# A fused attention and expert layer on one core: which pool holds the projection weights, and where the values stage keeps its gated units

## The chip, the cores and the metric

The kernel runs on one core of a Trainium2 chip. The metric is the time of one execution in microseconds (us). Times are compared as medians of several executions. Engines are named as the profile names them: PE (matmuls) with its weight loads PEld, DVE, ACT, POOL, and SP, which here only issues DMAs.

## The reference

One layer of an encoder is applied to two sequences, a prompt of 512 tokens and a sample of 256, with the same weights (width 1024):

```python
n = rms_norm(x, attn_norm_g)
proj = n @ w_in                    # q, k, v of 8 heads A and 4 heads B
o_a = dilated_attention(...)       # 8 heads of 64
o_b = diff_attention(...)          # 4 heads, two maps each, values of 128
x = x + concat(o_a, o_b) @ w_out
h = rms_norm(x, ffn_norm_g)
# expert layer: 128 * 128 experts of one neuron each
q  = h @ w_q                       # 8 heads, two halves of 128
sc = q . sub_keys                  # 128 scores per half, top 16 of each
best, pos = top_k(pairwise sums of the two lists, 16)
g = softmax(best)
x = x + sum over picks of g * gelu(h . u[e]) * v[e]
```

## The kernel before

Tokens are worked on in tiles of 128: four of the prompt (0 to 3), two of the sample (4, 5). fp32 products are made from three matmuls of split operands: `split` (L71 to L73) casts a raw tile to a rounded high part on ACT (L72) and subtracts it for the low part on POOL or DVE (L73), and `mm3` (L67 to L69) multiplies high by high, high by low and low by high. The stages, in the order in which they come:

1. Norm, input projection and attention of the sample, then of the prompt. `project` (L133) streams a weight matrix in pieces of 128x512 (`wraw`, split into `wh`, `wl`) from the pool `wpool`, three buffers of each.
2. The sample's output projection, its second norm, and its routing: `route_keys` and `route_pairs` find the 16 picks of each head by DVE operations. Routing of tiles 4 and 5 is scheduled beside the prompt's attention. Its last part (L515 to L527) lives in a pool `sr` on the left side: one-hot masks `ei`, `ej` (L491, L493), their sums (L522 to L525), and the expert numbers `eidx` (L526, L527).
3. The prompt's output projection: the first 512 columns of `w_out` by `project` (L536), accumulators `pacc` in four banks, added to the residual by `evac` (L292, DVE); then the other 512 columns from `woh`, `wol` (L541 to L545), second norm and transposes (L127) into `x2p`, two tiles of 16 KB per partition with the tags x0 and x1.
4. The prompt's routing, interleaved with the first `hidden` units: `hidden(j)` loads 128 experts' u vectors (`raw8`, L572), splits them, makes 24 matmuls `pu` with `x2p`, and writes the gelu to DRAM (`h_d`, L593).
5. The gate stage: dense gates of all prompt tokens and experts by one-hot matmuls `pg`, written to DRAM (`g_d`). Then the remaining `hidden` units.
6. The values stage (L677 on): 64 units of two experts' blocks. A unit reads `h_d` into `gw` (L684), multiplies it by gates `gblk` (L669, one 2 MB read for four units; L686), splits the product into `wh`, `wl` (the gated unit) and makes 96 matmuls `py` with two blocks of v. In the second unit the residual (`x1y`, 2 MB) is read back and added by transposes (L694 to L699).

Beside stages 4 to 6 the sample's picks are gathered row by row by POOL's DMAs, with DVE making the dot products (L722 to L732).

What sets the order: the program is written in stage order, and a scheduler that simulates a timeline places each instruction on its engine's queue. An engine's queue runs in order. Pools are stacks of memory, one growing from the left, one from the right; a tile of a pool that is opened where another pool has been closed waits, tile by tile, for the last instructions that used the memory below it. Before the change `wpool` is the upper pool on the right, open from the start until after stage 3. The values stage's pool `dp` (right) holds `gblk`, `gw`, `wh` and `wl`, and is opened at L663, where `wpool` and the prompt's pools have been closed.

Of the kernel before, what the change touches and what calls it, by code (L numbers as in the profile page):

```python
# [11 lines left out]
F32 = mybir.dt.float32  # L12
F32R = mybir.dt.float32r
# [8 lines left out]
P = 128  # L22
D = 1024
# [15 lines left out]
DENSE = 4  # L39
# [12 lines left out]
def tile_kernel(ctx, tc, xs_in, relb, onehot, logm, g1, w_in, gqk, lamv, gdiff, w_out, g2,  # L52
                w_q, skT, uT, uv, out_p, out_s, dbg=None):
    nc = tc.nc
    V, S, G, T = nc.vector, nc.scalar, nc.gpsimd, nc.tensor

    def f(ap):
        return ap.bitcast(F32)

    def pool(stack, name, bufs=1, side="left", **kw):  # L60
        return stack.enter_context(tc.tile_pool(name=name, bufs=bufs, side=side, reuse_waits="tile", **kw))

    def psum(stack, name, bufs):
        return stack.enter_context(tc.tile_pool(name=name, bufs=bufs, space=PSUM, reuse_waits="tile"))

    def mm3(ps, ah, al, bh, bl, start, stop):
        T.matmul(ps, ah, bh, start=start, stop=False)  # L67
        T.matmul(ps, ah, bl, start=False, stop=False)  # L68
        T.matmul(ps, al, bh, start=False, stop=stop)  # L69

    def split(hi, lo, raw, low=None):  # L71
        S.copy(hi, raw)  # L72
        return (low or G).tensor_tensor(lo, raw, f(hi), op=OP.subtract)  # L73
# [3 lines left out]
    late = pool(ctx, "late")  # L77
# [5 lines left out]
    ps_tr = psum(fps, "ps_tr", 1)  # L83
    ps_tr2 = psum(fps, "ps_tr2", 1)
    ps_mm = psum(fps, "ps_mm", 2)
    attm = ctx.enter_context(ExitStack())
    att = pool(attm, "att", 3)
    left = ctx.enter_context(ExitStack())
    ppS = pool(left, "ppS", 3)
    right = ctx.enter_context(ExitStack())  # L90
    ppP = pool(right, "ppP", 3, side="right")
    wpool = pool(right, "wpool", 3, side="right")

    def bank(p, name):
        return p.tile([P, 512], F32, tag="b", name=name)
# [182 lines left out]
    def mixed(n, mix, pp):  # L278
        mh = pp.tile([P, DC, n * P], F32R, tag="pj", name="mh")
        ml = pp.tile([P, DC, n * P], F32R, tag="pj", name="ml")  # L280
        for d in range(DC):
            split(mh[:, d], ml[:, d], mix[d // 4][:, d % 4], G if d < 4 else V)
        return mh, ml

    def residual(t0, n, pp):
        x1 = pp.tile([P, n, D], F32, tag="pj", name="x1")
        for i in range(n):
            nc.sync.dma_start(x1[:, i], xs_in[(t0 + i) * P:(t0 + i + 1) * P, :])

        def evac(i, nb, ps):  # L290
            c = slice(nb * 512, (nb + 1) * 512)
            V.tensor_tensor(x1[:, i, c], ps, x1[:, i, c], op=OP.add)  # L292

        return x1, evac
# [35 lines left out]
    for m in range(2):  # L330
        c = slice(m * 512, (m + 1) * 512)
# [195 lines left out]
        V.tensor_copy(eidx[t], ijf[:, 0])  # L527
    left.close()
    attm.close()


    rw = pool(ctx, "rw", 2)
    mh, ml = mixed(4, mixP, ppP)
    x1, evac = residual(0, 4, ppP)
    obanks = (ps_sc, ps_sc2, ps_tr, ps_tr2)
# [4 lines left out]
    for d in range(DC):  # L540
        raw = wpool.tile([P, 512], F32, name="wraw")  # L541
        nc.sync.dma_start(raw, w_out[d * P:(d + 1) * P, 512:])
        wh = wo.tile([P, 512], F32R, name="woh")
        wl = wo.tile([P, 512], F32R, name="wol")
# [22 lines left out]
    right = ctx.enter_context(ExitStack())  # L567
# [95 lines left out]
    dp = pool(ctx, "dense", 2, side="right")  # L663
    py = [ps_y.tile([P, 512], F32, name=f"py{c}") for c in range(DC)]
    vrows = uv.rearrange("(i j) d -> j i d", j=NK)

    def gates(jb):
        gblk = dp.tile([P, DENSE * P // TB, JB, TB], F32, name="gblk")
        nc.sync.dma_start(gblk, g_d[:, :, jb * JB:(jb + 1) * JB, :].rearrange("b i j t -> i b j t"))  # L669
        return gblk  # L670

    def values_of(j):
        vr, vh, vl = weights8(vrows[j, :, D:].rearrange("i (c d) -> i c d", d=P))
        low_of[NK + j] = split(vh, vl, vr, V)
        return vh, vl

    for jp in range(NK // 2):  # L677
        jj = 2 * jp % JB
        wh = dp.tile([P, 2, 512], F32R, name="wh")
        wl = dp.tile([P, 2, 512], F32R, name="wl")  # L680
        if jj == 0:
            gblk = gates(2 * jp // JB)
        ge = dp.tile([P, 2, 512], F32, name="gw", bufs=3)
        nc.sync.dma_start(ge, h_d[jp])  # L684
        ge4 = ge.rearrange("p k (b t) -> p k b t", t=TB)
        V.tensor_tensor(ge4, ge4, gblk[:, :, jj:jj + 2].rearrange("p b k t -> p k b t"), op=OP.mult)  # L686
        split(wh, wl, ge, V)
        vv = [values_of(2 * jp + k) for k in range(2)]
        for c in range(DC):
            for k, (vh, vl) in enumerate(vv):  # L690
                mm3(py[c], vh[:, c], vl[:, c], wh[:, k], wl[:, k],
                    jp == 0 and k == 0, jp == NK // 2 - 1 and k == 1)
        if jp == 1:
            x1y = late.tile([P, DENSE, D], F32, tag="x0", name="x1y")  # L694
            for t in range(DENSE):
                nc.sync.dma_start(x1y[:, t], x1_d[t])
            for c in range(DC):
                for t in range(DENSE):
                    T.matmul(py[c][:, t * P:(t + 1) * P], x1y[:, t, c * P:(c + 1) * P], ident, start=False, stop=False)  # L699
# [90 lines left out]
```

## Time and profile before

| | |
|---|---|
| median of 3 executions | 2289.11 us (2288.76 to 2289.37) |
| profiled execution | 2282.11 us, of it span 2280.3 us |
| PE busy | 2170.0 us, 95% of the span |
| DVE busy | 1800.5 us, 79% |
| ACT, POOL busy | 915.4 us (40%), 851.3 us (37%) |
| chain that ended last, by engine | PE 66%, DVE 10%, issue 8%, DMA 8%, POOL 5%, ACT 2% |
| DMA over the span | 617.65 MB, mean 271 GB/s |

The span runs from the first to the last instruction that the profiler recorded; the profiled execution's time is 1.8 us more than its span. The busy shares are averages over stages. Of the page's 40 slices of 57 us, PE is at 6 or 7 tenths in the first, the ninth and tenth (456 to 570 us) and the 25th (1368 to 1425 us), and at 8 or more in all others.

### The profile page before, as it was taken

What the parts mean: (1) busy time and instruction counts of PE and PEld (TensorE: products, weight loads), DVE (VectorE), ACT (ScalarE), POOL (GpSimd) and SP (SyncE); (2) the same over time, 40 slices, a digit from 0 to 9 for tenths busy, and PEclk for the clock granted to TensorE, in tenths of its full rate; (3) what the DMA queues carried; (4) which work ended last, traced back from release to release, by engine and by line L of the source; (5) the groups of instructions that cost most, each with busy time, mean ns of one, the idle gap of its engine ahead of it and who ended that gap; (6) DMA issues with size and microseconds to landing.
All of it is one profiled execution on the core that took longest, in us unless ns stands there. A gap on an engine that the chain in (4) does not pass through costs nothing.

```text
span 2280.3 us, 31093 instructions
## 1 busy us (share of the span) xinstructions
PE 2170.0 (95%) x11312; PEld 1770.3 (78%) x11312; DVE 1800.5 (79%) x3500; ACT 915.4 (40%) x1484; POOL 851.3 (37%) x634
## 2 busy tenths in 40 slices
PE   6999999976999989999999997999999999999998
PEld 4788789855887777878888875888878778788876
DVE  5645378997699999989999965666788878888885
ACT  4755587632322234545555532332223222223222
POOL 4767776632456532222322322221222322222320
PEclk9999999988999999999999998999999999999999
DMA  5533353314477776789998899898999999999994
GB/s 187 185 107 123 92 154 94 105 47 161 168 255 261 262 269 227 284 304 348 342 350 329 342 384 387 296 349 288 367 347 364 359 343 372 384 365 360 359 342 177
DMA packets 198681, 617.65 MB, mean 271 GB/s; under 512 B 16016, under 2 KB 82192, under 8 KB 163712
## 3 DMA queue, kind: packets, MB, share of 16 engines
q1 hardware_dynamic: 139968, 278.70, 35.2%
q0 software_dynamic: 36864, 268.45, 31.0%
q10 hardware_dynamic: 21696, 68.53, 7.8%
q8 instruction: 88, 1.44, 0.2%
q14 instruction: 65, 0.53, 0.1%
HBM read 542.17 MB, written 73.45 MB: 270 GB/s over the span
## 4 chain that ended last, share of the span: by engine, by line
PE 66%; DVE 10%; issue 8%; DMA 8%; POOL 5%; ACT 2%; SPq 0%; ACTq 0%; POOLq 0%; DVEq 0%
PE py L67 10%; PE py L68 10%; PE py L69 10%; PE pu L67 6%; PE pu L69 6%; PE pu L68 6%; DMA row<-in_uv_dram,eidx 3%; PE pacc L68 3%; PE pacc L69 3%; PE pacc L67 3%; POOL row L722 2%; DMA raw<-in_uT_dram 2%; PE pg L650 2%; PE pq L69 2%; POOL lo L73 1%
## 5 line engine op out<-in xcount | busy, mean ns | idle before, releaser
L722 POOL DMA_INDIRECT row<-in_uv_dram,eidx x256 | 413.6, 1616 | 1150.8 <-DVE acc L732 1011.1
L72 ACT CAST hi<-raw 128x1024 fp32r<-128x1024 f32 x272 | 285.1, 1051 | 571.7 <-PE pu L68 199.5
L67 PE MATMUL pu<-x2p,hi 128*128 128x512 f32 x1024 | 409.3, 400 | 15.7 <-ACT hi L72 15.6
L69 PE MATMUL pu<-x2p,lo 128*128 128x512 f32 x1024 | 408.5, 399 | 11.0 <-DVE lo L73 7.5
L67 PE MATMUL py<-wh,hi 128*128 128x512 f32 x1024 | 405.2, 396 | 2.6 <-ACT hi L72 2.6
L68 PE MATMUL pu<-x2p,hi 128*128 128x512 f32 x1024 | 406.5, 397 | 0.0
L73 DVE TENSOR_TENSOR lo<-raw,hi 128x1024 fp32r<-128x1024 f32 x236 | 287.7, 1221 | 149.4 <-ACT hi L72 112.5
L68 PE MATMUL py<-wl,hi 128*128 128x512 f32 x1024 | 404.2, 395 | 0.0
L724 DVE CUSTOM_DVE_ANT_0 row<-row,st 128x1024 f32<-128x1024 f32 x256 | 332.1, 1305 | 51.4 <-DMA row<-in_uv_dram,eidx 51.1
L732 DVE SCALAR_TENSOR_TENSOR acc<-row,wgt,acc 128x1024 f32<-128x1024 f32 x256 | 328.8, 1284 | 5.2
L69 PE MATMUL py<-wh,lo 128*128 128x512 f32 x1024 | 303.3, 395 | 0.0
L67 PEld LDWEIGHTS pu<-x2p,hi 128*128 128x128 f32 x1024 | 195.4, 191 | 58.7 <-ACT hi L72 16.9
L69 PEld LDWEIGHTS pu<-x2p,lo 128*128 128x128 f32 x1024 | 194.8, 190 | 55.1 <-DVE lo L73 12.2
L67 PEld LDWEIGHTS py<-wh,hi 128*128 128x128 f32 x1024 | 191.9, 187 | 53.8 <-ACT hi L72 6.9
L69 PEld LDWEIGHTS py<-wh,lo 128*128 128x128 f32 x1024 | 191.9, 187 | 46.9
L68 PEld LDWEIGHTS py<-wl,hi 128*128 128x128 f32 x1024 | 192.0, 187 | 46.3
L68 PEld LDWEIGHTS pu<-x2p,hi 128*128 128x128 f32 x1024 | 195.1, 191 | 38.6
L653 ACT COPY gb<-pg 128x512 f32<-128x512 f32 x128 | 132.7, 1146 | 81.8 <-PE pg L650 80.8
L73 POOL TENSOR_TENSOR wl<-wraw,wh 128x512 fp32r<-128x512 f32 x96 | 127.6, 1335 | 76.3 <-ACT wh L72 72.4
L72 ACT CAST wh<-gw 128x1024 fp32r<-128x1024 f32 x64 | 67.1, 1049 | 174.5 <-PE py L69 162.7
L729 ACT ACTIVATE wgt<-h 128x2 f32<-128x2 f32 x128 | 26.1, 204 | 220.6 <-DVE h L724 219.3
L650 PE MATMUL pg<-og,oij 128*128 128x128 bf16 x1536 | 110.0, 221 | 4.6 <-DVE og L643 4.6
(303 smaller groups left out, 3659.7 us busy)
## 6 DMA issues: line engine op xcount, KB each, us to landing
raw<-in_uT_dram SPq DMA_DIRECT2D x128, 512.0 KB, 5.9
raw<-in_uv_dram SPq DMA_DIRECT2D x128, 512.0 KB, 7.9
h_d<-ge ACTq DMA_DIRECT2D x128, 256.0 KB, 5.6
g_d<-gb ACTq DMA_DIRECT2D x16, 2048.0 KB, 9.4
gblk<-g_d SPq DMA_DIRECT2D x16, 2048.0 KB, 16.5
gw<-h_d SPq DMA_DIRECT2D x64, 512.0 KB, 9.1
wraw<-in_w_in_dram SPq DMA_DIRECT2D x96, 256.0 KB, 2.8
toe<-bias_d SPq DMA_DIRECT2D x24, 448.0 KB, 4.1
```

Source lines behind the costliest of these rows:

```text
L67: T.matmul(ps, ah, bh, start=start, stop=False)
L68: T.matmul(ps, ah, bl, start=False, stop=False)
L69: T.matmul(ps, al, bh, start=False, stop=stop)
L72: S.copy(hi, raw)
L73: return (low or G).tensor_tensor(lo, raw, f(hi), op=OP.subtract)
L650: T.matmul(pg[:, c], oij[:, 0, c4 * 4 + c], og[k][:, c4 * 4 + c], start=k == 0, stop=k == 2)
L653: S.copy(gb[:, :, o:o + 4].rearrange("p j t -> p t j"), pg)
L722: G.indirect_dma_start(out=r, out_offset=None, in_=uv, in_offset=bass.IndirectOffsetOnAxis(ap=eidx[t][:, b + k:b + k + 1], axis=0))
L724: dot = V.tensor_tensor_reduce(r[:, :D], r[:, :D], x2r[t], 1.0, 0.0, OP.mult, OP.add, h[:, k:k + 1])
L729: S.activation(wgt, h, AF.Gelu)
L732: V.scalar_tensor_tensor(acc, rows[k][:, D:], wgt[:, k:k + 1], acc, op0=OP.mult, op1=OP.add)
```

## The change

The diff has three parts.

- `wpool` moves from the right side to the left. It is opened before the attention's pool `att`, in a stack of its own (`wx`) that is closed after `attm`. The prompt's output projection uses a new pool, `wout`, which is opened on the right after the pool `rw`, with the same buffers.
- The gated units of the values stage no longer have tiles of their own in `dp` (two buffers each of `wh` and `wl`). They take the halves `[:, jp % 2]` of two tiles `w0`, `w1`, which have the tags x0 and x1, the buffers of `x2p`.
- `x1y`, which had the tag x0, is now a tile of `dp`.

```diff
     ps_mm = psum(fps, "ps_mm", 2)
+    wx = ctx.enter_context(ExitStack())
+    wpool = pool(wx, "wpool", 3)
     attm = ctx.enter_context(ExitStack())
     att = pool(attm, "att", 3)
...
     ppP = pool(right, "ppP", 3, side="right")
-    wpool = pool(right, "wpool", 3, side="right")
...
     left.close()
     attm.close()
+    wx.close()
...
     rw = pool(ctx, "rw", 2)
+    wpool = pool(right, "wout", 3, side="right")
     mh, ml = mixed(4, mixP, ppP)
...
     for jp in range(NK // 2):
         jj = 2 * jp % JB
-        wh = dp.tile([P, 2, 512], F32R, name="wh")
-        wl = dp.tile([P, 2, 512], F32R, name="wl")
+        wh, wl = (late.tile([P, 2, 2, 512], F32R, tag=f"x{i}", name=f"w{i}") for i in range(2)) if jp == 0 else (wh, wl)
...
-        split(wh, wl, ge, V)
+        gh, gl = wh[:, jp % 2], wl[:, jp % 2]
+        split(gh, gl, ge, V)
...
-                mm3(py[c], vh[:, c], vl[:, c], wh[:, k], wl[:, k],
+                mm3(py[c], vh[:, c], vl[:, c], gh[:, k], gl[:, k],
                     jp == 0 and k == 0, jp == NK // 2 - 1 and k == 1)
         if jp == 1:
-            x1y = late.tile([P, DENSE, D], F32, tag="x0", name="x1y")
+            x1y = dp.tile([P, DENSE, D], F32, name="x1y", bufs=1)
```

Line numbers of the changed kernel are higher by 1 from L94 on, by 3 from L533 on, and by 2 or 3 in the values stage. Below, the names are those of the program; the number behind a name is that of the buffer.

ACT's queue at the end of the prompt's attention, before. `mh` is the last mixed head, `wh` the pieces of `w_out`, `hi8` the first blocks of stage 4, `gate5` the sample's second routing (tile 5):

```order
L72 CAST mh_6406<-mixP_2957 128x512
L72 CAST wh_6489<-wraw_6487 128x512
L72 CAST hi8_6859<-raw8_6857 128x1024
L72 CAST wh_6507<-wraw_6505 128x512
L72 CAST hi8_6893<-raw8_6891 128x1024
L72 CAST wh_6525<-wraw_6523 128x512
L72 CAST wh_6543<-wraw_6541 128x512
L463 ACTIVATE gate5_5201<-gate5_5201 128x128
L72 CAST wh_6561<-wraw_6559 128x512
L72 CAST woh_6586<-wraw_6584 128x512
```

The same place of ACT's queue now:

```order
L72 CAST mh_6410<-mixP_2957 128x512
L72 CAST hi8_6863<-raw8_6861 128x1024
L72 CAST hi8_6897<-raw8_6895 128x1024
L464 ACTIVATE gate5_5201<-gate5_5201 128x128
L72 CAST wh_6439<-wraw_6437 128x512
L72 CAST wh_6457<-wraw_6455 128x512
L72 CAST wh_6475<-wraw_6473 128x512
L72 CAST wh_6493<-wraw_6491 128x512
```

Before, three `wh` stand far ahead of these rows, four between `mh` and `gate5`, and one behind it; now all eight stand behind `gate5`. PE's queue follows: of the 96 matmuls `pacc<-wh,mh` and the like, 27 stood between the matmuls of the last attention head, and now all 96 stand behind its last transpose (L271, now L272). On DVE the four `wol` subtractions and the four residual additions of the first half stood among the routing of tile 5; now they stand behind its last operation.

SP's queue with what each DMA waits for, the first pieces of `w_out` now. A wait names the engine or the DMA queue whose count is waited for:

```order
L575 DMA raw8_7003<-in_uT_dram 128x1024 [waits DMAHW6_49,DMAHW3_49,Pool_49]
L575 DMA raw8_7038<-in_w_q_dram 128x8x128 [waits DMAHW7_49,DMAHW4_49,Pool_49]
L140 DMA wraw_6437<-in_w_out_dram 128x512 [waits DMAHW0_49,DVE_49]
L140 DMA wraw_6455<-in_w_out_dram 128x512 [waits DMAHW1_49,PE_49]
L140 DMA wraw_6473<-in_w_out_dram 128x512 [waits DMAHW2_49]
L140 DMA wraw_6491<-in_w_out_dram 128x512 [waits DMAHW0_49,Pool_49]
```

Before, the pieces waited for POOL alone (the subtraction that frees a buffer), and the first six were loaded during the attention. In the compiled program the count of DVE that `wraw_6437` waits for is that of L494 (L493 before), the multiplication of tile 5's `ej`; the first cast `wh_6439` waits for L526 (L525 before) and the second for L528 (L527), the sum and the last cast of the same tile.

SP's queue at the end of the gate stage before, where the values stage's first reads go out between the blocks of the hidden units:

```order
L669 DMA gblk<-g_d 128x16x256
L684 DMA gw<-h_d 128x1024 x3
L669 DMA gblk<-g_d 128x16x256
L572 DMA raw_14332<-in_uT_dram 128x1024
L572 DMA raw_14366<-in_uT_dram 128x1024
L572 DMA raw_14400<-in_uT_dram 128x1024
L684 DMA gw<-h_d 128x1024 x2
L572 DMA raw_14434<-in_uT_dram 128x1024
L572 DMA raw_14468<-in_uT_dram 128x1024
L572 DMA raw_14502<-in_uT_dram 128x1024
L669 DMA gblk<-g_d 128x16x256
L572 DMA raw_14536<-in_uT_dram 128x1024
```

And now:

```order
L672 DMA gblk<-g_d 128x16x256
L686 DMA gw<-h_d 128x1024 x2
L699 DMA x1y<-x_d_97 128x1024
L699 DMA x1y<-x_d_98 128x1024
L699 DMA x1y<-x_d_99 128x1024
L699 DMA x1y<-x_d_100 128x1024
L686 DMA gw<-h_d 128x1024
L575 DMA raw_14336<-in_uT_dram 128x1024
L672 DMA gblk<-g_d 128x16x256
L575 DMA raw_14370<-in_uT_dram 128x1024
L575 DMA raw_14404<-in_uT_dram 128x1024
L575 DMA raw_14438<-in_uT_dram 128x1024
```

Two `gw` and the third `gblk` move from here to behind the first blocks of v; the four reads of `x1y` came from there. The casts of the first two gated units stood on ACT among the hidden units; now they stand behind the last gelu, and in the compiled program the cast of the third unit still waits for the last matmul of the first.

## Rows read from the trace of the kernel before

**Rows 1.** busy time of the engines, from the page

```profile
PE 2170.0 (95%) x11312; PEld 1770.3 (78%) x11312; DVE 1800.5 (79%) x3500; ACT 915.4 (40%) x1484; POOL 851.3 (37%) x634
```

**Rows 2.** PE's timeline, 474 to 557 us: start, length, engine, line, operation, [idle before]

```profile
474.35 0.80 PE L67 MATMUL pacc<-wh,mh 128*128 128x512 f32 x1 [2.41 <-DVE mx L195]
...
521.38 1.68 PE L67 MATMUL pacc<-wh,mh 128*128 128x512 f32 x4 [2.63 <-ACT wh L72]
...
532.66 0.77 PE L67 MATMUL pacc<-woh,mh 128*128 128x512 f32 x1 [6.40 <-DVE x L292]
...
553.64 0.40 PE L67 MATMUL pacc<-woh,mh 128*128 128x512 f32 x1
...
556.21 0.40 PE L69 MATMUL pacc<-woh,ml 128*128 128x512 f32 x1
```

**Rows 3.** DVE's timeline, the sample's routing, 470 to 543 us

```profile
470.04 0.45 DVE L470 CAST tb<-ti 128x256 bf16<-128x256 uint32 x1
...
497.95 0.27 DVE L468 TENSOR_TENSOR gate<-gate,gr 128x128 f32<-128x128 f32 x1
...
503.00 1.20 DVE L493 TENSOR_TENSOR ej<-ej,tb 128x2048 bf16<-128x2048 bf16 x1
...
506.43 2.49 DVE L470 CAST tb<-ti 128x256 bf16<-128x256 uint32 x1
...
523.21 2.29 DVE L493 TENSOR_TENSOR ei<-ei,di 128x2048 bf16<-128x2048 bf16 x1
...
538.74 2.21 DVE L493 TENSOR_TENSOR ej<-ej,tb 128x2048 bf16<-128x2048 bf16 x1
540.99 1.48 DVE L524 TENSOR_TENSOR ej<-ej 128x1024 bf16<-128x1024 bf16 x3
542.50 0.29 DVE L525 TENSOR_TENSOR ijf<-ej 128x128 f32<-128x128 bf16 x1
```

**Rows 4.** PE's waits, 1340 to 1430 us: total, times, longest

```profile
PE pu L67 <- ACT hi L72: 15.6, 3, 6.1
```

**Rows 5.** windows: length, busy PE, PEld, DVE, ACT, POOL (instructions), PE clock, DMA share, GB/s

```profile
1350.00:1390.00 40.00, 28.21 (x107) 21.57 (x107) 23.92 (x29) 10.42 (x15) 6.63 (x4) 0.87 1.04 399
1420.00:1430.00 10.00, 4.28 (x10) 2.81 (x10) 3.85 (x7) 2.15 (x4) 0.00 (x0) 0.66 0.78 290
1430.00:1500.00 70.00, 70.00 (x311) 57.95 (x310) 48.29 (x58) 21.78 (x33) 20.65 (x13) 1.00 0.86 325
```

**Rows 6.** ACT's timeline, one cast at 521 us, two operations near 1550 us

```profile
520.72 0.60 ACT L72 CAST wh<-wraw 128x512 fp32r<-128x512 f32 x1
...
1543.19 0.59 ACT L592 ACTIVATE ge<-pu 128x512 f32<-128x512 f32 x1
...
1555.14 1.05 ACT L72 CAST wh<-gw 128x1024 fp32r<-128x1024 f32 x1
```

**Rows 7.** DVE by line, 500 to 544 us: count, busy us, mean ns, idle before

```profile
L524 DVE TENSOR_TENSOR ej<-ej 128x1024 bf16<-128x1024 bf16 (+2 forms) x6 | 5.5, 915 | 0.1
...
L73 DVE TENSOR_TENSOR wol<-wraw,woh 128x512 fp32r<-128x512 f32 x4 | 2.9, 736 | 1.1 <-ACT woh L72 1.1
L292 DVE TENSOR_TENSOR x<-pacc,x 128x512 f32<-128x512 f32 x4 | 2.5, 676 | 0.0
...
L525 DVE TENSOR_TENSOR ijf<-ej 128x128 f32<-128x128 bf16 x2 | 1.5, 762 | 0.0
...
L468 DVE TENSOR_TENSOR gate<-gate,gr 128x128 f32<-128x128 f32 x1 | 1.3, 1316 | 0.0
```

**Rows 8.** POOL's timeline, 505 to 524 us

```profile
505.92 2.85 POOL L73 TENSOR_TENSOR lo<-raw,hi 128x1024 fp32r<-128x1024 f32 x1
...
521.40 1.74 POOL L73 TENSOR_TENSOR wl<-wraw,wh 128x512 fp32r<-128x512 f32 x1 [6.24 <-ACT wh L72]
```

**Rows 9.** DMA issues, 500 to 545 us: KB each, us to landing

```profile
wraw<-in_w_out_dram SPq DMA_DIRECT2D x10, 256.0 KB, 2.7
```

**Rows 10.** window of the second half, same columns

```profile
532.60:556.60 24.00, 23.94 (x96) 18.95 (x96) 11.40 (x19) 2.36 (x5) 4.00 (x3) 0.94 0.26 99
```

## The prediction

> **What bounds the kernel now.** First the page: PE is busy for 2170.0 of 2280.3 us [rows 1], so PE's queue sets the end nearly everywhere, and the question is where the change adds idle time on PE or takes some away. The profiled execution took 2282.1 us, 7.0 less than the median of 2289.1; I make the sum against 2282.1 and add 7.0 at the end. Then PE's timeline around the place where the diff moves `w_out`. The reader is to see three things in it [rows 2]: at 474.35 us PE already makes matmuls of the prompt's output projection in a gap of the attention (it had idled 2.41 us for DVE); the first half still runs at 521.38, after a small wait for ACT; the second half starts at 532.66, after 6.40 us of waiting for the residual additions on DVE, and its last matmul starts at 556.21 and ends at 556.6. Then DVE in the same stretch: it works through the sample's routing, and the last multiplication of tile 5's `ej` starts only at 538.74 [rows 3]. Last come the waits and windows at the end of the gate stage, where PE waits 15.6 us for casts of blocks that are late [rows 4, 5], and ACT around 1543 to 1555 us, where the hidden units end [rows 6].
>
> **Part one: the output projection behind the routing (slower).** The new pool `wout` lies on memory of the sample's routing. The first `wraw` now waits for DVE's multiplication of tile 5's `ej`; SP's queue stands behind it, and ACT's first `wh`, POOL's `wl` and all 192 matmuls `pacc` come after. Queued behind the waiting read on SP are the other pieces and then stage 4's reads, five blocks of which stand ahead of it; behind ACT's waiting cast are the pieces and the norm of the same stage. So only this stage waits. Before, the weights waited for no part of the routing. So I need the end of that multiplication in the new order.
>
> It ended at 538.74 + 2.21 = 540.95 [rows 3]. Ahead of it stood four `wol` subtractions (2.9 us and 1.1 us of waiting for ACT) and four residual additions (2.5 us), 6.5 us in all [rows 7], which now come after it. That alone gives 534.45.
>
> Besides, DVE operations of the routing take longer while POOL makes its low parts: the multiplications of L493 at 523.21 and 538.74 took 2.29 and 2.21 us against 1.20 at 503.00; the six additions of L524 took 5.5 us together, where three at 540.99, with POOL quiet, took 1.48; L525 1.5 for two against 0.29 for one; L468 1.3 against 0.27 [rows 3, 7]. Over the undisturbed durations that is 2.1 + 2.5 + 0.9 + 1.0 = 6.5 us. POOL's `wl` and `wol`, as the one at 521.40 [rows 8], go behind the routing with the weights, so I take these 6.5 us off too: 527.9. Bounds: nothing comes off (534.45), or 2.0 more does, if the cast at 506.43 (2.49 us against 0.45 at 470.04 [rows 3]) is freed of the `lo` of 505.92 [rows 8], which stays on POOL: 525.9.
>
> [...]
>
> From there: 2.7 us for the `wraw` to land [rows 9]; 0.6 us for the cast of `wh` [rows 6]; PE starts at 531.2. A half of the projection, 96 matmuls, took 23.94 us with its slow start after a wait [rows 10]; so I take the first half from 531.2 to 555.1, since the pieces (cast 0.6, POOL below 2 us, three buffers) come faster than twelve matmuls, some 2.9 us, use them up. One of the four additions, 0.63 us [rows 7], is exposed before the second half. The second half runs warm: the twelve matmuls from 553.64 to 556.21 start 0.234 us apart [rows 2], so 96 take 22.4 us. The end is 555.1 + 0.6 + 22.4 = 578.1 against 556.6: **21.5 us later**, bounds 19.5 and 28. PE idles from the end of the attention to 531 and nothing else is on its queue: the 27 matmuls that filled gaps of the last head fill none now. What follows (norm, transposes, prompt's routing) begins with the last matmul of this stage, so it shifts as a whole.
>
> **Part two: fewer early reads at the end of the gate stage (faster, small).** In full-speed stretches a matmul slot is 70/311 = 0.225 us. From 1350 to 1390 us there were 107, so 40 − 107 × 0.225 = 15.9 us were lost, and from 1420 to 1430 10 − 10 × 0.225 = 7.7 us [rows 5], part of it at a granted clock of 0.87 and 0.66 of full speed. The DMA rate there is 399 GB/s, at a busy share of 1.04 [rows 5], so what the early reads cost is their bytes. Before, these were three `gblk` and five `gw`, 8.5 MB; now they are two `gblk`, three `gw` and `x1y`, 7.5 MB. One MB less at 399 GB/s is 2.5 us: **2.5 us earlier**. Ahead of the first block stand 5.5 MB both times, so the first loss stays. The bounds: the 7.7 us behind the third `gblk` go whole, or nothing is won, since the two `gw` and the `gblk` now go out at the start of the values stage, with 1 MB more than `x1y` there, worth 2.5 us if that stretch waits for DMA: −7.7 to +2.5.
>
> **Part three: hidden to values (slower, small).** `w0` lies on `x2p`, so the first gated unit is cast only after the last `pu`. The last gelu, 0.59 us, stands before the cast of 1.05 us on ACT [rows 6], and PE waits for both: **1.6 us later**. The low part on DVE is hidden behind the first eight matmuls with the high part. Bounds 0 (the gelu's wait hides behind a wait for a block) and 5 (the stage begins with three gated reads instead of five in hand). In the steady stage the halves take turns as the two buffers did: the cast of a unit waits for the matmuls two units back, as before; cost nothing, hidden behind a unit of 96 matmuls.
>
> **Sum.** 21.5 − 2.5 + 1.6 = 20.6; 2282.1 + 20.6 + 7.0 = 2309.7 us.
>
> **Rivals.**
> Routing with no relief: DVE's lengthening is not POOL's doing, `ej` ends at 534.45, and part one costs 28. Then 2316. For it: most lengthened rows are of tile 5, whose data may differ; against it the three quick additions at 540.99, of tile 5 too [rows 3].
>
> Not slower: the wait for the routing decides nothing. Place: the first `wraw`. Price nil if the multiplication of `ej` ends before 527.9 − 21.5 = 506.4; the point from which it costs is there. Then 2282.1 − 2.5 + 1.6 + 7.0 = 2288.2, and faster by over 0.2% only if part two also wins its 7.7 (2283). Against it: in DVE's queue the routing of tile 5 can't be done at 506, where DVE is only at its first cast [rows 3].
>
> The early reads win everything: both losses of part two, 23.6 us, go, and the time is 2288.6, no change. For it: the third `gblk` is gone from there; against it: 5.5 MB still stand ahead of the first block.
>
> The values stage loses its lead: with fewer gated reads in hand, and 3 MB of reads at its start, its first units wait for theirs. At 5 us for each of two units it is 10 us: 2320. For it: the reads are larger there than before; against it: they are behind the first five blocks of v, and used two units, over 20 us, later. That the halves do not do what they say (a unit waiting for the other half's matmuls) would add a cast, 1.05 us, to each of 62 units, 2375; the waits in the program speak against it.
>
> **How the numbers follow.** Forecast 0.70, for 2303 to 2315; no relief 0.12; values stage worse 0.08; halves 0.01; not slower at the projection 0.05; early reads win all 0.04. The range holds the forecast and the no-relief case, with some of the values case: 2299 to 2320. About 0.2% (4.6 us) is what a measurement of this kernel can tell from no change; of the last two cases faster by more gets 0.04 and within it 0.05, the others are slower, 0.91.
>
> **What would show it.** In the profile of the changed kernel: the first `pacc` with `wh` at about 531 (no earlier than 3 us after L494 of tile 5), PE idle for over 25 us before it, and the last with `woh` near 578; DVE's L494 and L525 of tile 5 near 1.2 us and 1.5 us for three; PE's wait for the cast of `hi` near 1420 gone and that near 1370 not; one wait of about 1.6 us at the first `py`; and no new waits in the values stage. I am wrong if `pacc` begins before 515, or if PE waits in the values stage exceed 5 us.

## The result

The changed kernel took 2303.82 us (median of 7 runs, 2298.21 to 2314.86), the kernel before 2289.11 (7 runs, 2283.25 to 2292.93). The ratio is 1.0069, with a 95% interval of 1.0046 to 1.0091: by the ratio slower by 16 us, between 10.5 and 21. The forecast was 2309.7 us, range 2299 to 2320.

The profiled execution of the changed kernel took 2314.86 us, the longest of its seven. Its span was 32.7 us longer than that of before, twice the difference of the medians, so a second profile was taken (e12 below, 2304.79 us). Where PE stood at the ends of the stages in the two kernels, read from PE's timeline (us from the span's start):

| | last `woh` matmul ends | last `pg` ends | last `pu` ends | first `py` | last `py` ends | span |
|---|---|---|---|---|---|---|
| before | 556.6 | 1333.6 | 1542.4 | 1542.3 | 2271.6 | 2280.3 |
| changed, first profile | 577.1 | 1359.0 | 1571.8 | 1574.1 | 2304.2 | 2313.0 |
| changed, second profile | 574.8 | 1351.3 | 1565.4 | 1567.8 | 2294.2 | 2303.0 |

The output projection costs 20.5 us in the first and 18.2 in the second profile, the hidden stage 4.0 and 5.3, the step from `pu` to `py` 2.5, and the values stage +0.8 and −2.9. The stretch between the projection and the last `pg` differs by 4.9 and −0.5, in which I see the spread of single executions. Counted from the end of the attention's last transposes (500.3 us before, 503.1 and 500.8 after), the projection ends 56.3 us later before, and 74.0 us later in both profiles after: 17.7 us more.

The page after, whose lines answer to [rows 1]: PE has lost 11 us of busy time, though it makes the same matmuls.

```profile
span 2313.0 us, 31093 instructions
...
PE 2159.4 (93%) x11312; PEld 1779.3 (77%) x11312; DVE 1791.0 (77%) x3500; ACT 915.4 (40%) x1484; POOL 835.9 (36%) x634
```

PE's timeline after, the lines that answer to [rows 2]: one wait of 26.66 us stands between the last transpose of the attention and the first matmul of the projection, and the 96 matmuls of a half follow one another.

```profile
501.99 1.12 PE L272 MATMUL pt<-ident,on 128*128 128x128 f32 x4 [9.15 <-DVE on L269]
529.76 2.08 PE L67 MATMUL pacc<-wh,mh 128*128 128x512 f32 x4 [26.66 <-ACT wh L72]
...
554.45 0.50 PE L67 MATMUL pacc<-woh,mh 128*128 128x512 f32 x1 [0.29 <-DVE x L293]
...
576.72 0.40 PE L69 MATMUL pacc<-woh,ml 128*128 128x512 f32 x1
```

DVE's and POOL's timelines after, which answer to [rows 3] and [rows 8]. The multiplication of tile 5's `ej` (L494 now) takes 1.23 us, not 2.21; the first `wl` waits for the cast of 529.1. Beside the two `lo` at 505.50 other operations are stretched than before: L526 takes 2.29 us there, and 0.29 at 527.66.

```profile
503.90 0.29 DVE L471 CAST tb<-ti 128x256 bf16<-128x256 uint32 x1
...
505.98 2.29 DVE L526 TENSOR_TENSOR ijf<-ej 128x128 f32<-128x128 bf16 x1
...
508.41 2.21 DVE L527 SCALAR_TENSOR_TENSOR ijf<-ijf 128x128 f32<-128x128 f32 x1
...
524.89 1.23 DVE L494 TENSOR_TENSOR ej<-ej,tb 128x2048 bf16<-128x2048 bf16 x1
526.15 1.48 DVE L525 TENSOR_TENSOR ej<-ej 128x1024 bf16<-128x1024 bf16 x3
527.66 0.29 DVE L526 TENSOR_TENSOR ijf<-ej 128x128 f32<-128x128 bf16 x1
```

```profile
505.50 4.97 POOL L73 TENSOR_TENSOR lo<-raw,hi 128x1024 fp32r<-128x1024 f32 x2 [6.49 <-ACT hi L72]
529.79 3.75 POOL L73 TENSOR_TENSOR wl<-wraw,wh 128x512 fp32r<-128x512 f32 x3 [19.31 <-ACT wh L72]
```

PE's waits after, 1340 to 1600 us, which answer to [rows 4]: four waits for casts of blocks, not three, and two new ones at the start of the values stage.

```profile
PE pu L67 <- ACT hi L72: 18.5, 4, 10.4
PE py L67 <- ACT w L72: 2.3, 1, 2.3
PE pu L69 <- DVE lo L73: 1.5, 1, 1.5
PE py L68 <- DVE w L73: 1.1, 1, 1.1
```

At that start ACT casts a block of v ahead of the last gelu, and DVE makes two dot products of the sample's gathers ahead of the first low part `w` (ACT's timeline, then DVE's; the lines answer to [rows 6]):

```profile
1571.56 1.04 ACT L72 CAST hi<-raw 128x1024 fp32r<-128x1024 f32 x1 [3.90 <-PE pu L68]
1572.51 0.59 ACT L595 ACTIVATE ge<-pu 128x512 f32<-128x512 f32 x1
1573.00 1.04 ACT L72 CAST w<-gw 128x1024 fp32r<-128x1024 f32 x1
```

```profile
1573.78 1.22 DVE L727 CUSTOM_DVE_ANT_0 row<-row,st 128x1024 f32<-128x1024 f32 x1
...
1574.93 1.22 DVE L727 CUSTOM_DVE_ANT_0 row<-row,st 128x1024 f32<-128x1024 f32 x1
...
1576.07 2.35 DVE L73 TENSOR_TENSOR w<-gw,w 128x1024 fp32r<-128x1024 f32 x2
```

Windows of 100 us in the values stage (columns as in [rows 5]), before and then after. Before, 428 matmuls take 99.75 us of PE's time, 0.233 each. After, a window almost without waits has 437 in 99.44, 0.228 each; the one ahead of it holds 409, since PE idles 5.5 us there.

```profile
1600.00:1700.00 100.00, 99.75 (x428) 79.86 (x427) 78.96 (x92) 28.68 (x35) 24.29 (x16) 1.00 0.96 352
```

```profile
1700.00:1800.00 100.00, 94.54 (x409) 77.36 (x408) 78.25 (x91) 28.03 (x34) 24.79 (x17) 0.98 0.93 356
1800.00:1900.00 100.00, 99.44 (x437) 81.38 (x436) 82.73 (x96) 29.01 (x36) 26.97 (x17) 1.00 0.96 366
```

PE's waits from 1700 us to the end after: 15.4 us for casts of blocks, where the kernel before had 1.7 in the same part.

```profile
PE py L67 <- ACT hi L72: 15.4, 12, 5.2
```

### The profile page after: what moved, and what is told of

It is laid out like the page before. It is cut to its first block, busy times and chain, and to the rows that moved or that the text cites. A ratio compares the mean times of both kernels' runs of the same rounds, so it can differ in the third digit from the quotient of the medians.

```text
span 2313.0 us, 31093 instructions
## 1 busy us (share of the span) xinstructions
PE 2159.4 (93%) x11312; PEld 1779.3 (77%) x11312; DVE 1791.0 (77%) x3500; ACT 915.4 (40%) x1484; POOL 835.9 (36%) x634
## 4 chain that ended last, share of the span: by engine, by line
PE 64%; DMA 12%; DVE 10%; issue 8%; POOL 4%; ACT 2%; SPq 0%; ACTq 0%; POOLq 0%; DVEq 0%
PE py L67 8%; PE py L68 8%; PE py L69 8%; PE pu L67 6%; PE pu L69 6%; PE pu L68 6%; DMA raw<-in_uv_dram 4%; PE pacc L68 3%; DMA row<-in_uv_dram,eidx 3%; PE pacc L69 3%; PE pacc L67 3%; POOL row L725 2%; DMA wraw<-in_w_in_dram 2%; PE pg L653 2%; PE pq L69 2%
## 5 line engine op out<-in xcount | busy, mean ns | idle before, releaser
L725 POOL DMA_INDIRECT row<-in_uv_dram,eidx x256 | 399.0, 1559 | 1179.3 <-DVE acc L735 1041.8
L67 PE MATMUL py<-w,hi 128*128 128x512 f32 x1024 | 400.9, 393 | 18.4 <-ACT hi L72 15.9
L68 PE MATMUL py<-w,hi 128*128 128x512 f32 x1024 | 400.4, 391 | 1.1 <-DVE w L73 1.1
L69 PE MATMUL py<-w,lo 128*128 128x512 f32 x1024 | 294.2, 389 | 0.4 <-DVE lo L73 0.4
L67 PEld LDWEIGHTS py<-w,hi 128*128 128x128 f32 x1024 | 193.2, 189 | 66.1 <-ACT hi L72 23.6
L68 PEld LDWEIGHTS py<-w,hi 128*128 128x128 f32 x1024 | 193.4, 189 | 41.4 <-DVE w L73 1.6
L69 PEld LDWEIGHTS py<-w,lo 128*128 128x128 f32 x1024 | 192.1, 188 | 40.7 <-DVE lo L73 0.8
L72 ACT CAST w<-gw 128x1024 fp32r<-128x1024 f32 x64 | 67.0, 1049 | 168.4 <-PE py L69 167.7
L72 ACT CAST wh<-wraw 128x512 fp32r<-128x512 f32 x120 | 74.4, 623 | 104.0 <-DMA wraw<-in_w_in_dram 38.7
```

Of the source, the lines that this page charges most:

```text
L725: G.indirect_dma_start(out=r, out_offset=None, in_=uv, in_offset=bass.IndirectOffsetOnAxis(ap=eidx[t][:, b + k:b + k + 1], axis=0))
```

## The experiments

Ratios are to the kernel before on the same chip in the same hours.

**e3, the first part alone** (`wpool` on the left, `wout` on the right; values stage as before).

```diff
+    wx = ctx.enter_context(ExitStack())
+    wpool = pool(wx, "wpool", 3)
...
-    wpool = pool(right, "wpool", 3, side="right")
...
+    wx.close()
     rw = pool(ctx, "rw", 2)
+    wpool = pool(right, "wout", 3, side="right")
```

> Only the first part of the change: projection weights on the left, the output projection's on the right behind the attention; the values stage as before. Theory of the prediction: the first matmul of the output projection with wh waits until about 530, and the whole time is 20 us above before, less 2 to 4 us of faster input projection: 2305 to 2310; py stays at 0.234. If the loss lies elsewhere: 2289 within 5.

2309.59 us, ratio 1.0090 (1.0069 to 1.0110): +20.6 us by the ratio. PE's timeline has the wait (26.75 us), and the projection ends at 573.5 against 556.6, 16.9 us later (18.4 counted from the end of the attention). In this profile the values stage is longer too, 735.2 us against 729.3, so that not all of the 20.6 need be the projection's:

```profile
525.56 2.08 PE L67 MATMUL pacc<-wh,mh 128*128 128x512 f32 x4 [26.75 <-ACT wh L72]
```

**e4, the changed kernel with `wout` on the left.**

```diff
     rw = pool(ctx, "rw", 2)
-    wpool = pool(right, "wout", 3, side="right")
+    wox = ctx.enter_context(ExitStack())
+    wpool = pool(wox, "wout", 3)
...
-    wox = ctx.enter_context(ExitStack())
     wo = pool(wox, "wo", DC)
```

> The changed kernel, with the pool of the output projection's weights opened on the left, below wo, so that it lies on memory of the attention and not of the sample's routing. Theory of the prediction: the first wraw no longer waits for the multiplication of tile 5's ej; the projection starts soon after the attention, 0 to 8 us later than before (no pieces ahead of time), and the whole time is 12 to 20 us below the changed kernel: 2284 to 2292. If the wait for the routing was not the cause: 2304 within 4.

2287.46 us, ratio 0.9991 (0.9970 to 1.0012), 16 us below the changed kernel. PE's timeline: the wait is 1.95 us, and the projection ends at 564.0, 7.4 us behind before. With e3 this shows the wait for the routing to be what makes the changed kernel slow: it comes with the place of the pool, and goes with it.

```profile
506.14 2.07 PE L67 MATMUL pacc<-wh,mh 128*128 128x512 f32 x4 [1.95 <-ACT wh L72]
...
539.05 0.80 PE L67 MATMUL pacc<-woh,mh 128*128 128x512 f32 x1 [7.40 <-DVE x L293]
...
561.01 0.40 PE L67 MATMUL pacc<-woh,mh 128*128 128x512 f32 x1
...
563.58 0.40 PE L69 MATMUL pacc<-woh,ml 128*128 128x512 f32 x1
```

**e2, the second and third part alone** (gated units in `w0`, `w1`, `x1y` in `dp`; the first part of the diff undone).

> Only the second and third part of the change: gated units in the halves of w0 and w1, x1y in dp; the projection weights stay on the right as before. Theory of the prediction: no wait at the output projection, so the 20.5 us go; the start of the values stage costs 1.6 to 2.5, and py has 0.227 us slots as in the changed kernel. By the address pair or the place: 2272 to 2288. If the loss of the changed kernel came from the values stage, this one is slower than before, 2300 or more.

2284.69 us, ratio 0.9986 (0.9969 to 1.0003): 3 us less than before, just not clear of no change. Its profile has both sides: the values stage from first to last `py` takes 722.8 us in place of 729.3, the hidden stage from last `pg` to last `pu` 212.6 in place of 208.8, and the step between them 2.3 us. From 1580 us on PE waits 9.5 us for blocks, 2.2 before.

**e1, 32 bytes on the right.** The tiles' addresses showed that everything on the right side starts at 32 modulo 64 bytes per partition, and everything on the left at 0. So `py` had a moving operand at 163808 (32) and a stationary one at 79552 (0); now both are at 0, as `pu`'s always were. The question was whether that sets the rate.

```diff
+    edge = pool(ctx, "edge", side="right")
+    V.memset(edge.tile([P, 8], F32, name="pad"), 0.0)
     right = ctx.enter_context(ExitStack())
```

> The kernel before with one unused tile of 32 bytes per partition at the outer end of the right side, so that every tile on the right starts 32 bytes lower (wh of the values stage at 163776 instead of 163808 per partition, a multiple of 64). Nothing else changes. Theory address pair: a matmul is slower (0.234 us a slot against 0.227) when its moving and its stationary operand stand 32 bytes apart modulo 64; then py runs at 0.227 here, the projections too, and up to 20 us of the values stage and 5 us of the projections can be won, less what the blocks of v then come late: 2268 to 2286. Theory place: the rate comes from the tile on the left side (or its shape), not from the address; then py stays at 0.234 and the time at 2289 within 3.

2275.46 us, ratio 0.9935 (0.9915 to 0.9955): by the ratio 15 us faster than before, and faster than the changed kernel. Window of the values stage, and two of the last twelve matmuls of the output projection: 0.227 us for a `py`, and (554.68 − 552.18) / 11 = 0.227 for a `woh`, which took 0.234 before [rows 2] and takes (563.58 − 561.01) / 11 = 0.234 in e4, where `woh` is at 0 and `mh` at 32.

```profile
1600.00:1700.00 100.00, 99.16 (x437) 81.46 (x436) 83.18 (x94) 28.96 (x35) 28.55 (x18) 1.00 0.96 361
```

```profile
552.18 0.39 PE L67 MATMUL pacc<-woh,mh 128*128 128x512 f32 x1
...
554.68 0.39 PE L69 MATMUL pacc<-woh,ml 128*128 128x512 f32 x1
```

Of the 20 us that 3072 matmuls could win in the values stage, its profile shows none: PE waits 16.4 us there for late blocks, and first to last `py` takes 731.2 us. The profiled execution, 2280.32 us, was the slowest of e1's six; in which stages the median gains, one profile does not show.

```profile
PE py L67 <- ACT hi L72: 16.4, 11, 6.6
```

**e6, 32 bytes on the left**, so that both sides stand at 32.

```diff
+    V.memset(const.tile([P, 8], F32, name="pad"), 0.0)
     ident = const.tile([P, P], F32, name="ident")
```

> The kernel before with one unused tile of 32 bytes per partition at the start of the left side: every tile on the left moves up by 32 bytes, those on the right stay, so that both sides now stand at 32 modulo 64. Theory address pair (only the difference of the two operands counts): py, the input and output projections run at 0.227 us a slot, the time is that of the pad on the right, 2270 to 2282. Theory absolute address (an operand at 32 modulo 64 is slow by itself): now pu and pq, which ran at 0.227 with both operands at 0, run at 0.234 too, the hidden stage grows by some 20 us, and the time is 2300 to 2315.

2274.54 us, ratio 0.9947 (0.9929 to 0.9965), the same as e1. Its windows: 440 `py` in 99.72 us, 0.227, and in the hidden stage 267 `pu` in 60 us, where the kernel before has 266. The values stage takes 725.0 us. So an operand at 32 is not slow by itself; what counts is that the two stand alike.

```profile
1440.00:1500.00 60.00, 60.00 (x267) 49.70 (x266) 42.39 (x52) 18.89 (x29) 17.20 (x11) 1.00 0.87 332
1600.00:1700.00 100.00, 99.72 (x440) 82.32 (x439) 82.25 (x94) 29.16 (x35) 25.41 (x16) 1.00 0.97 361
```

**e7, `x1y` read late** (e2, with the four reads held behind the second unit's blocks in SP's order).

```diff
-                nc.sync.dma_start(x1y[:, t], x1_d[t])
+                back = nc.sync.dma_start(x1y[:, t], x1_d[t])
+                tc.add_manual_dep(back.ins, low_of[NK + 3].ins.name, NOSYNC, reason="order")
```

> Only the values part of the change, as in e2, with the four reads of x1y held behind the second unit's blocks of v in the order of SP's queue. Theory bytes: the early reads cost the hidden stage their bytes; 2 MB less make it 5 us shorter than in e2 (last pg to last pu 212.6 us there), about 207.5, and the time is 2279 to 2284. Theory order (what costs is that the first block waits behind a gw that waits for gblk to land): the hidden stage stays at 211 to 213 and the time at 2285 within 3.

2289.82 us, ratio 1.0004 (0.9990 to 1.0019), outside both forecasts. The hidden stage is 205.4 us, 7.2 less than in e2, as the theory of bytes has it. But the edit took away more than bytes: the third `gw` no longer waits for `gblk`, and PE's first wait for a block is 4.13 us, where e2 has 10.36. That is 6.2 of the 7.2 us (see part two below), so this run does not show that the bytes cost them. The values stage takes 738.4, 15.6 more than in e2, with 19.3 us of waits for blocks against 9.5.

**e8 and e9, half the gathers' bytes**, with the pad (e8) and without (e9).

```diff
-                G.indirect_dma_start(out=r, out_offset=None, in_=uv,
+                G.indirect_dma_start(out=r[:, :D], out_offset=None, in_=half_rows,
...
-                V.scalar_tensor_tensor(acc, rows[k][:, D:], ...
+                V.scalar_tensor_tensor(acc, rows[k][:, :D], ...
```

> The kernel before with the pad on the right, and the sample's gathers at half their bytes: each pick reads 4 KB in place of 8 KB from a view of half rows, and the same half stands for u and for v, so the sample's output is not the reference's. Theory DMA: with py at 0.227 the values stage is at the limit of the DMA queues, and its waits for late blocks of v (16 us in the profile of e1) take the gain back; at half the gathers they fall below 3 us, the stage from first to last py takes 704 to 710 us in place of 731, and the time is 2245 to 2260. Theory order of the queue (blocks of v are issued late whatever the load): waits stay above 10 us and the time at 2268 to 2276.

> The kernel before, without the pad, with the same half gathers (the sample's output is not the reference's). By both theories the values stage is bound by PE at 0.234 us a slot and has only 2.6 us of waits to give back: the stage stays at 725 to 729 us and the time at 2275 to 2289, so that the distance to e8 is 20 us or more by the theory of DMA and under 15 by the theory of order.

2375.74 us (1.0427, 1.0382 to 1.0473) and 2383.45 us (1.0449, 1.0411 to 1.0487): both far slower, and inconclusive. The scheduler wrote another order of DVE's operations; the waits of PE in e8's values stage, below, are for DVE's subtractions, 75 us, and DVE itself waits there, from 1600 to 2200 us, 73.6 us for gathered rows and 71.8 for `gw`. PE's waits for ACT's casts of late blocks are 1.9 us, but with PE slower they would be few anyway.

```profile
PE py L69 <- DVE lo L73: 64.3, 40, 3.9
PE py L68 <- DVE wl L73: 10.4, 7, 2.2
PE py L67 <- ACT hi L72: 1.9, 2, 1.1
```

**e10 and e11, four pairs of gathers moved** from the values stage to the hidden units, with the pad (e10) and without (e11).

```diff
-    early += [low_of[FIRST_GATHER + k * span // rest] for k in range(rest)]
+    spots = [FIRST_GATHER + k * span // rest for k in range(26)]
+    spots += [91 + k * 37 // 22 for k in range(22)] + [128 + k * 128 // 56 for k in range(rest - 48)]
+    early += [low_of[j] for j in spots]
```

> The kernel before with the pad on the right, and four of the sample's 128 pairs of gathers moved from the values stage to the hidden units 91 to 127 (22 pairs there in place of 18, 56 in place of 60 from unit 128 on); all work is done. Theory DMA load: with py at 0.227 us a slot the values stage is late by what its reads take; 8.4 MB fewer there at some 357 GB/s are up to 23 us of DMA time, so its waits of 16 us fall below 6 and the time to 2262 to 2271, 5 to 12 below the pad alone (2275). Theory order (the blocks are late by their place in the queue, not by load): 2273 to 2279.

> The kernel before without the pad, with the same four pairs of gathers moved. By both theories its values stage runs at PE's 0.234 us a slot and has some 3 us of waits to give back, and the hidden stage may lose as much: 2284 to 2290. If it falls as far as e10 does against the pad alone, the load held up the kernel before as well.

2292.24 us (1.0033, 1.0021 to 1.0045) and 2310.52 us (1.0119, 1.0099 to 1.0139). Both miss their forecasts: with the move the hidden stage takes 214.8 and 212.1 us and the values stage 733.5 and 746.3. The theory of load is not borne out: with fewer gathers there, PE still waits 16.4 us for blocks in e10's values stage, and 12.1 in e11's. It is not refuted either. In the traces the stage holds 112 gathers in place of e1's 116, so about 4 MB moved and not the 8.4 that were meant, and DVE's operations come in another order than in e1. The pad is worth 18 us between the two.

**e12, the changed kernel again.**

> The changed kernel once more, for a second profile, since the first one is of the slowest of its runs. By the sum of parts: last matmul of the output projection some 20 us behind before, the hidden stage (last pg to last pu) 212 to 213 us, first py 2.3 to 3.5 us after the last pu, py at 0.227 us a slot, and waits for blocks of v of 8 to 16 us in the values stage; 2300 to 2310.

2304.79 us. Its stages are in the table at the top; PE waits 11.5 us for casts of blocks in the values stage, and at its start 2.3 us for the cast of `w` and 0.3 for its low part.

**e13, four buffers for the blocks** (e1, with one buffer of `acc` given for it).

```diff
-        raw = rw.tile([P, DC, P], F32, name="raw8", bufs=3)
+        raw = rw.tile([P, DC, P], F32, name="raw8", bufs=4)
...
-        acc = gp.tile([P, D], F32, name="acc")
+        acc = gp.tile([P, D], F32, name="acc", bufs=1)
```

> The kernel before with the pad on the right, four buffers for the streamed blocks (raw8) in place of three; the memory comes from one buffer of acc in place of two. All work is done. Theory buffers: blocks of v come late when a 2 MB gblk stands ahead of them, and a fourth buffer sends them 5.4 us earlier; PE's waits in the values stage fall from 16 us to below 6 and those at the end of the gate stage by some 5, so 2258 to 2270 against 2275 of the pad alone. Theory rate (the queues can't move the bytes faster, however early they are asked for): the waits stay above 12 us and the time within 4 of 2275.

2291.16 us, ratio 1.0036 (1.0010 to 1.0061), slower than e1 and outside both forecasts. In the stages it was meant for, the numbers go the way of the theory of buffers: hidden stage 202.4 us against 209.0 in e1, first to last `py` 716.9 against 731.2, waits for blocks 8.9 us against 16.4. But the projection ends 6.3 us later, the stretch to the last `pg` takes 8.8 us more, and at the end the span runs 20.9 us past the last `py`, against 8.8: the sample's last gathers come after it. Which of the two edits causes these losses was not separated, and since the order of DVE's operations changed as well, the gains are not shown to be the fourth buffer's alone. PE's waits in e13's values stage, and then DVE's timeline after the last `py`, where the dot products wait for gathered rows:

```profile
PE py L67 <- ACT hi L72: 8.9, 11, 2.2
```

```profile
2268.55 1.23 DVE L726 CUSTOM_DVE_ANT_0 row<-row,st 128x1024 f32<-128x1024 f32 x1 [1.15 <-DMA row<-in_uv_dram,eidx]
...
2272.68 1.22 DVE L726 CUSTOM_DVE_ANT_0 row<-row,st 128x1024 f32<-128x1024 f32 x1 [2.90 <-DMA row<-in_uv_dram,eidx]
```

## Why the prediction came out right, and where it was wrong

**Part one held in mechanism; its size came out somewhat smaller.** Forecast: `ej` ends at 527.9, first matmul at 531.2, the projection 21.5 us late, 19.5 at least. First profile: 526.1, 529.8, 20.5; second: 523.8, 527.5, 18.2; e3: 521.8, 525.6, 16.9. Two of the three delays are under the lower bound. Counted from the end of the attention it is 17.7 to 18.4 us in all three. The relief was the uncertain term, and it came: L494 1.23 us, three additions of L525 1.48, all with POOL quiet, as the bound with relief had it. The rival without relief (2316) falls. No term had the prompt's input projection, which took 161.6 us in the first profile in place of 164.7; its slot is treated below.

Where POOL is still busy, two of DVE's operations are lengthened in the first profile: L526 at 505.98, an operation of 0.29 us, ended at 508.27, and L527 at 510.62, each about when one of the two `lo` of 2.5 us ended (4.97 us from 505.50 for both). What in the chip lengthens them, no run shows.

**Part two had the wrong sign.** Forecast: 2.5 us earlier, with the first loss as before and the one behind the third `gblk` gone. Measured: the hidden stage 4.0 and 5.3 us longer in the changed kernel, 3.8 and 3.7 in e2 and e4, and not in e3 (0.5). PE's waits for casts of blocks, before and then after:

```profile
1371.79 0.79 PE L67 MATMUL pu<-x2p,hi 128*128 128x512 f32 x1 [3.80 <-ACT hi L72]
...
1385.46 0.79 PE L67 MATMUL pu<-x2p,hi 128*128 128x512 f32 x1 [6.15 <-ACT hi L72]
...
1425.86 0.79 PE L67 MATMUL pu<-x2p,hi 128*128 128x512 f32 x1 [5.69 <-ACT hi L72]
```

```profile
1398.05 0.80 PE L67 MATMUL pu<-x2p,hi 128*128 128x512 f32 x1 [10.42 <-ACT hi L72]
...
1422.85 0.79 PE L67 MATMUL pu<-x2p,hi 128*128 128x512 f32 x1 [6.20 <-ACT hi L72]
...
1444.20 0.50 PE L67 MATMUL pu<-x2p,hi 128*128 128x512 f32 x1 [1.62 <-ACT hi L72]
```

They come 38, 52 and 92 us after the last `pg` before, and 39, 64 and 85 us after it now. So the last one shrank, by 4 us, and the middle one stayed (8.42 us in the second profile). The step that failed is "the first loss stays", which rested on the 5.5 MB that stand ahead of the first block both times: the first wait grew from 3.80 to 10.42 us. It is not set by these bytes. ACT's timeline at this place, before and then after (in brackets, with what ended the wait):

```profile
1370.33 0.33 ACTq L593 DMA_DIRECT2D h_d<-ge  x1
1370.70 1.04 ACT L72 CAST hi<-raw 128x1024 fp32r<-128x1024 f32 x1 [7.51 <-DMA gblk<-g_d]
```

```profile
1396.58 0.33 ACTq L596 DMA_DIRECT2D h_d<-ge  x1
1396.95 1.05 ACT L72 CAST hi<-raw 128x1024 fp32r<-128x1024 f32 x1 [14.13 <-DMA gw<-h_d]
...
1421.75 1.04 ACT L72 CAST hi<-raw 128x1024 fp32r<-128x1024 f32 x1 [9.90 <-DMA raw<-in_uT_dram]
```

Ahead of the late cast in ACT's queue stands the write of a gelu to `h_d`, and in the compiled program this write waits for an earlier read that uses the same DMA count. Before, that is the first `gblk`. Now it is the second `gw`, which lands behind the `gblk`, and the write that is held is that of one unit earlier. So ACT stands 14.13 us in place of 7.51. That is 6.6 us more, and PE's wait grew by the same 6.6. In e7 the write waits for `gblk` again, ACT stands 7.84 us, and PE's wait is 4.13. No run changed this count alone, so it is shown by the program and the timelines, not by an experiment of its own. The middle wait has another cause now: the second `gblk` goes out right behind the first block, and the next cast waits 9.90 us for its block.

**Part three had the right place and about half the size.** Forecast 1.6; the two waits are 2.3 and 1.1 us in the first profile, 2.3 and 0.3 in the second. The cast of a block of v ahead of the gelu, about 0.8 us, and the two dot products ahead of DVE's low part were not in my sum: I took the eight matmuls with the high part to hide the subtraction, which waited for its engine instead.

**The steady values stage was not "cost nothing".** The prediction said that it is wrong if PE's waits in the values stage exceed 5 us, and here it was: 15.9 and 11.5 us of waits for blocks in the changed kernel from 1580 us on, 2.2 before. Its rival of a lost lead is not what happened, since nearly all of these waits come after the first units. The slot went from 0.234 to 0.227 us, which no step of mine had, although [rows 2] and [rows 5] held both rates side by side: `woh` at 0.234, `pu` at 0.225. Over 3072 matmuls (48 in each of the 64 units, where the prediction has 96) that is 21 us, and most of it went into the waits: in e1, whose operations in this stage come in the order of the kernel before, they are 16.4 us. The waits understate the loss. Counted from start to start of the matmuls, what goes beyond 0.23 us in slots of over 0.3 us is 25.7 and 22.1 us in the changed kernel and 26.8 in e1, against 5.4 before. Why the blocks come late is not settled: e8, e10 and e13 changed the order of the operations along with the load and the buffers.

**The sum.** By the ratios the two halves alone are +20.6 (e3) and −3 (e2), the whole +16. The forecast was 5.9 us too high in the median. In the hidden stage and at the step it lacked some 8 us of cost; the projection, the values stage and the input projection, which cost less than forecast or gave time back, made up for it. How much each gave the profiles do not say: single executions differ by several us, and that of the kernel before lay 7.0 below its median. Being right rests on part one; that the other errors nearly cancelled is luck.

## What to carry to other kernels

Moving a pool moves its waits: look at which tiles lay on its new memory before, and at when the last of their users comes in its engine's queue, for that is when the first tile can be filled (in the first profile here PE idled 26.66 us for it). Compare the slot of one kind of matmul with another's in the same profile; where equal shapes run at two rates (here 0.227 and 0.234 us), look at the operands' addresses. A DMA that an engine issues can hold the work behind it in that engine's queue (here ACT stood 14.13 us), so where a cast is late, look at what the DMA just ahead of it waits for. A faster engine shows the next bound: of 21 us won on PE's rate, the profiles of the padded kernels gave the values stage none (e1) and 4 us (e6), because the blocks were not there (waits of 16.4 and 14.4 us for their casts).

## What the runs showed of the hardware

A 128x128 by 128x512 fp32 matmul in a dense run took 0.227 us when its moving and its stationary operand started at the same address modulo 64 bytes (both at 0: `pu` in all kernels but e6, `py` in e1; both at 32: `py` and `pu` in e6), and 0.234 when one stood at 0 and the other at 32 (`py` before and in e3, `woh` with `mh` before and in e4). One stage of the kernel before shows both: in the prompt's output projection the median from start to start is 0.227 in the first half, with `wh` and `mh` both at 32, and 0.234 in the second. In e4, where `wh` is at 0, the first half has 0.232. The granted clock was 1.00 in the windows of 1600 to 1700 us at either rate, before and in e1. The difference, 3%, is worth 12 to 15 us of this kernel for 32 bytes of padding (ratios 0.9947 and 0.9935). Only the offsets 0 and 32 were tried; what in the chip makes the difference was not.
